# A diffusion block on one core: front reordered, stores and loads moved between queues, SiLU by Sigmoid

## The chip, the core and the metric

The kernel runs on one core of a Trainium2 chip. The metric is the device time of one execution in microseconds (us), as the median over several runs. Five engines take instructions, each strictly in its own order: PE (TensorE: matmuls, with PEld for its weight loads), DVE (VectorE: elementwise work), ACT (ScalarE: activations, casts, copies), POOL (GpSimd) and SP (SyncE, which here only issues DMAs). SP, ACT and POOL each issue DMAs into a queue of their own.

## What is computed

One layer over 512 latent tokens `x` and 256 context tokens, width 1024, fp32:

```python
m_lat = (silu(c) @ mod_w + mod_b)                  # 6 sections of 1024: sh1, sc1, g1, sh2, sc2, g2
m_ctx = (silu(c_ctx) @ mod_w + mod_b)
h_lat = rms_norm(x, g) * (1 + sc1) + sh1           # the same for ctx with csc1, csh1
qkv, a, beta, g_a, q_b, i_b, f_b, g_b, m_a, m_b = split(h @ w_in)
# mixer A: gated DeltaNet, 4 heads; mixer B: HGRN2, 4 heads; both directions, chunks of 64;
# each scan starts from the final context state
ya = (head_norm(oa) * silu(g_a)) @ w_up_a
yb = (head_norm(ob) * silu(g_b)) @ w_up_b
x = x + g1 * ((sigmoid(m_a) * ya + sigmoid(m_b) * yb) @ w_out)
x = x + g2 * swiglu(rms_norm(x) * (1 + sc2) + sh2, ffn_w_in, ffn_w_out)
return rms_norm(x, final_norm_g)
```

## The kernel before

Everything has features on the 128 partitions and tokens along the free axis. A product with full precision is three fp32r matmuls: `split` loads 128 columns of a weight as `raw` (L92, SP's queue), casts them to `hi` on ACT (L100) and takes `lo = raw - hi` on DVE (L102); `mm3` (L110) then runs hi·hi, hi·lo and lo·hi over the blocks of the contraction.

The program is written with the Tile framework: buffers come from pools with rings (`bufs`), waits are derived from data and from rings, and each engine's order follows the place in the code, moved by `tc.cur_priority`. The stages, with the times at which they stand in the profiled execution:

- Front (0 to 95 us). `x` is loaded and normed. `modulation(q)` (L279 to L293) works on two 128-feature blocks of shift and scale at a time: 16 matmuls `pmod` on two tiles `mw` (1 MB each, L279), a copy `mr` to SBUF (L282), four matmuls with `comb` that turn the rows into columns (L284), and three small DVE operations into `mcol`. For each feature block d, `px` transposes the normed rows (L299), ACT writes `hhi` (L301) and `hf` (L303) from it, and DVE `hlo` (L304). The first six M_B gates are accumulated over d in six banks `pg` (L330, weights `wr` loaded whole by SP). Then come `gate_out` for those six, two more gates (22 and 23, `pgate`), the context's `chi`, `clo` (px in the banks "ga"), and `pab` (L375), the small projections on the context.
- `gate_out` (L136, L137) copies a gate's bank to `gt` on ACT and stores it to DRAM (`gdram`) through SP's queue; the ring of `gt` has two buffers.
- Mixer (95 to 605 us). Eight generators are stepped by the string `PLAN`: G0 and G2 (DeltaNet, two heads each), H0 to H3 (HGRN2), F (a gate between them), and N or aT, one quarter of a later modulation section: `mod_early` loads 1 MB `mwe` through POOL's queue, reduces it over the eight k-blocks on DVE (L851 to L854) and sums over partitions with `column_sums` (L116, 16 matmuls). What PLAN does not place comes as `mod_quarter` (`mwb`, POOL's queue) near the end of the mixer. The heads' outputs are stored to `ydram` (L439) on SP's queue.
- Merge (605 to 720 us, its first loads from 582 us). `branch(br)` loads the gate `ug` and the head output `uy` (SP), takes SiLU on ACT (L956), multiplies on DVE (L959), splits into `yh`, `yl`. `up` multiplies with w_up (`pup`), loads the merge gate `mg` (SP, same ring "ug" of four buffers), takes its Sigmoid (L974) and multiplies with the bank (L976).
- FFN (720 to 1080 us), which the change does not touch.

## Time and profile before

| | |
|---|---|
| median of 3 runs | 1079.61 us (1078.65 to 1081.12) |
| the profiled execution | 1081.61 us, span 1079.6 us, granted TensorE clock 0.99 |
| PE, DVE, ACT, POOL busy | 94%, 61%, 51%, 7% of the span |
| DMA traffic | 122 MB, 113 GB/s on average, 290 to 329 GB/s in the first 54 us |

The profiled execution is one of its own; durations below come from it. The views used are the page (busy time, the chain of waits that ended last, groups of instructions, DMA issues), the windows (busy time of each engine in given stretches), the timeline (instructions in order of time, with the idle time ahead of each in brackets and what ended it) and the waits (who waited for whom, total, times, longest). "128*32" ahead of a matmul is the part of the array used.

### The profile page before, as it was taken

To read this page: it belongs to the slowest core of one execution; us is meant where nothing else is said; L and a number is where in the kernel's file an instruction comes from. 1 tells how busy PE (TensorE), PEld (TensorE's weight loads), DVE (VectorE), ACT (ScalarE), POOL (GpSimd) and SP (SyncE) were. 2 spreads that over 40 slices of the span, in tenths; PEclk is the share of its full clock that TensorE was granted. 3 is DMA by queue.
4 is the path that set the end of the run, shared out by engine and by line. 5 is a ranking of instruction groups with operands and counts; after the bars stand their busy time and mean duration, and the time that the engine had idled before them with its cause. 6 is when DMAs were issued, how large, how long until landed. Compare 5 with 4: busy or idle time off the path is not lost.

```text
span 1079.6 us, 16501 instructions
## 1 busy us (share of the span) xinstructions
PE 1014.1 (94%) x6455; PEld 839.9 (78%) x6455; DVE 656.5 (61%) x1238; ACT 554.5 (51%) x1042; POOL 76.6 (7%) x133
## 2 busy tenths in 40 slices
PE   4999999979999999999999899999999999999996
PEld 2686788858897877789777688797888878888785
DVE  3336886789867967976797565776343433422524
ACT  3456578748976765887774643442222222221212
POOL 1010000320002022000201000010000000000000
PEclk8999999999999999999999999999999999999999
DMA  9953412122004213200738743455333323322222
GB/s 329 290 168 91 138 55 65 54 79 59 3 11 147 64 45 88 59 2 22 241 112 280 239 159 120 137 158 174 98 97 96 96 85 98 97 97 96 86 95 95
DMA packets 134529, 122.07 MB, mean 113 GB/s; under 512 B 5533, under 2 KB 110259, under 8 KB 134451
## 3 DMA queue, kind: packets, MB, share of 16 engines
q1 hardware_dynamic: 127715, 100.20, 29.9%
q0 software_dynamic: 4640, 17.30, 4.9%
q10 hardware_dynamic: 2096, 3.50, 0.9%
q8 instruction: 51, 0.84, 0.3%
q14 instruction: 27, 0.22, 0.1%
HBM read 110.51 MB, written 10.49 MB: 112 GB/s over the span
## 4 chain that ended last, share of the span: by engine, by line
PE 60%; DVE 13%; DMA 9%; ACT 7%; issue 7%; POOL 3%; SPq 0%; POOLq 0%; ACTq 0%; DVEq 0%
PE pf L110 20%; PE pfo L110 10%; PE pg L330 3%; PE pup L110 3%; PE h_z L110 3%; PE pgate L110 2%; DMA mwb<-in_mod_w_dram 2%; DVE lo L102 2%; DMA mwe<-in_mod_w_dram 2%; PE h_zv L110 2%; DMA ug<-gdram 1%; ACT hi L100 1%; DMA gdram<-gt 1%; PE p_s_pk L801 1%; PE g_k_zl L110 1%
## 5 line engine op out<-in xcount | busy, mean ns | idle before, releaser
L100 ACT CAST hi<-raw 128x1024 fp32r<-128x1024 f32 (+1 forms) x131 | 129.7, 991 | 279.9 <-PE pf L110 97.3
L102 DVE TENSOR_TENSOR lo<-raw,hi 128x1024 fp32r<-128x1024 f32 (+1 forms) x131 | 150.5, 1150 | 172.6 <-ACT hi L100 172.2
L110 PE MATMUL pf<-hhi,lo 128*128 128x512 f32 (+1 forms) x352 | 133.8, 380 | 0.8 <-DVE lo L102 0.8
L110 PE MATMUL pf<-hhi,hi 128*128 128x512 f32 (+1 forms) x352 | 133.8, 381 | 0.0
L110 PE MATMUL pf<-hlo,hi 128*128 128x512 f32 (+1 forms) x352 | 133.7, 380 | 0.0
L110 PEld LDWEIGHTS pf<-hhi,lo 128*128 128x128 f32 x352 | 66.2, 188 | 13.7 <-DVE lo L102 1.2
L110 PEld LDWEIGHTS pf<-hlo,hi 128*128 128x128 f32 x352 | 66.2, 188 | 12.5 <-DVE hlo L1042 0.2
L110 PEld LDWEIGHTS pf<-hhi,hi 128*128 128x128 f32 x352 | 66.1, 188 | 12.5
L110 PE MATMUL pfo<-lo,uh 128*128 128x512 f32 x176 | 68.8, 391 | 0.1
L110 PE MATMUL pfo<-hi,ul 128*128 128x512 f32 x176 | 68.5, 389 | 0.0
L110 PE MATMUL pfo<-hi,uh 128*128 128x512 f32 x176 | 67.9, 390 | 0.0
L110 PE MATMUL pgate<-hhi,lo 128*128 128x512 f32 x144 | 59.2, 412 | 6.5 <-DVE lo L102 6.5
L110 PE MATMUL pgate<-hhi,hi 128*128 128x512 f32 x144 | 59.2, 411 | 2.3 <-ACT hi L100 2.3
L110 PE MATMUL pgate<-hlo,hi 128*128 128x512 f32 x144 | 58.2, 404 | 0.0
L1098 DVE TENSOR_TENSOR sg<-sg,pf 128x512 f32<-128x512 f32 x22 | 15.1, 687 | 49.3 <-PE pf L110 49.3
L835 DVE SCALAR_TENSOR_TENSOR acc<-mwb,sc,acc 128x256 f32<-128x256 f32 x72 | 34.5, 484 | 12.4 <-DMA mwb<-in_mod_w_dram 11.2
L110 PEld LDWEIGHTS pfo<-lo,uh 128*128 128x128 f32 x176 | 33.0, 188 | 7.8 <-DVE lo L102 1.0
L110 PEld LDWEIGHTS pfo<-hi,uh 128*128 128x128 f32 x176 | 32.8, 188 | 7.4 <-ACT hi L100 0.7
L110 PEld LDWEIGHTS pgate<-hhi,lo 128*128 128x128 f32 x144 | 27.8, 193 | 13.8 <-DVE lo L102 8.9
L110 PE MATMUL h_z<-hhi,hi 128*128 128x512 f32 x96 | 38.1, 397 | 0.4 <-ACT abT L376 0.3
L110 PEld LDWEIGHTS pfo<-hi,ul 128*128 128x128 f32 x176 | 33.0, 188 | 6.8
L110 PE MATMUL h_z<-hhi,lo 128*128 128x512 f32 x96 | 38.0, 396 | 0.0
(443 smaller groups left out, 2498.3 us busy)
## 6 DMA issues: line engine op xcount, KB each, us to landing
raw<-in_ffn_w_in_dram SPq DMA_DIRECT2D x44, 512.0 KB, 3.7
raw<-in_w_in_dram SPq DMA_DIRECT2D x37, 512.0 KB, 3.7
raw<-in_ffn_w_out_dram SPq DMA_DIRECT2D x22, 512.0 KB, 3.6
mwb<-in_mod_w_dram POOLq DMA_DIRECT2D x18, 512.0 KB, 4.6
mw<-in_mod_w_dram SPq DMA_DIRECT2D x16, 512.0 KB, 6.0
mwe<-in_mod_w_dram POOLq DMA_DIRECT2D x7, 1024.0 KB, 6.1
gdram<-gt SPq DMA_DIRECT2D x24, 256.0 KB, 3.3
raw<-in_w_in_dram SPq DMA_DIRECT2D x18, 256.0 KB, 2.9
```

Source lines behind the costliest of these rows:

```text
L100: nc.scalar.copy(hi[:, :, :], raw[:, :, :])
L102: nc.vector.tensor_tensor(lo[:, :, :], raw[:, :, :], hi.bitcast(F32), op=ALU.subtract)
L110: nc.tensor.matmul(ps, a[u](k), b[v](k), start=(start and n == 0), stop=(stop and n == tot - 1))
L330: nc.tensor.matmul(pg0[i][:, :], u[:, P * i:P * i + P], v[:, d, :], start=(d == 0 and n == 0), stop=(d == KT - 1 and n == 2))
L801: nc.tensor.matmul(pk[:, 2 * P:3 * P], kend[:, :], u[:, :], start=True, stop=True)
L835: nc.vector.scalar_tensor_tensor(acc[:, :], mw[:, k - k0, :], sc[:, k:k + 1], acc[:, :], op0=ALU.mult, op1=ALU.add)
L1098: nc.vector.tensor_tensor(sg[:, :], sg[:, :], pgu[1][:, :], op=ALU.mult)
```

## The change

1. Modulation comes in five groups of blocks, (0), (1), (2,3), (4,5), (6,7). The first two have one 1 MB tile with all eight k-blocks and 512-byte rows; the `comb` matmuls are four times as many, on 32 columns each. The `wr` loads stand between them.
2. Gates 22 and 23 stand behind the context's norm and `pab` in the code, with priority lowered (`+1500`) and weight tiles of their own. The context's `px` uses the banks "ha"; for odd d its `hf` is made on DVE.
3. Four quarters of the modulation that PLAN had at its start are computed in the front by `mod_now`, loaded by SP into the `mw` ring.
4. The 24 gate stores and the 8 head-output stores are issued by ACT. The `gt` ring has three buffers in the front.
5. The loads `ug` and `mg` are issued by POOL, and `mg` has a ring of four of its own.
6. SiLU is `gt*yt` on DVE, Sigmoid on ACT, and a second product on DVE.
7. The mask `lev` comes as uint8 (112 KB in place of 448) and needs no cast on ACT.

```diff
-PLAN = ("H0:1 aT:1 N:1 aT:2 G0:6 F:1 H1:3 G0:4 F:1 G2:3 G0:5 F:2 N:1 G0:1 H0:2 "
+PLAN = ("H0:1 G0:6 F:1 H1:3 G0:4 F:1 G2:3 G0:5 F:2 N:1 G0:1 H0:2 "
...
         def gate_out(i, ps, pool, tag="raw"):
-            gt = pool.tile([P, SEQ], F32, name=f"gt{i}", tag=tag, bufs=2)
+            gt = pool.tile([P, SEQ], F32, name=f"gt{i}", tag=tag, bufs=3 if pool is ring.get("sp") else 2)
             nc.scalar.copy(gt[:, :], ps[:, :])
-            nc.sync.dma_start(gdram[i, :, :], gt[:, :])
+            nc.scalar.dma_start(gdram[i, :, :], gt[:, :])
...
+        def mod_now(sec, j, mw, queue):
+            c0 = D * sec + 256 * j
+            queue.dma_start(mw[:, 0:KT, :], T["mod_w"][0, :, c0:c0 + 256].rearrange("(k p) f -> p k f", p=P))
+            for k in range(KT):
+                acc = mw[:, k % 2, :]
+                if k < 2:
+                    nc.vector.tensor_scalar_mul(acc, acc, sc[:, k:k + 1])
+                else:
+                    nc.vector.scalar_tensor_tensor(acc, mw[:, k, :], sc[:, k:k + 1], acc, op0=ALU.mult, op1=ALU.add)
+            nc.vector.tensor_tensor(mw[:, 0, :], mw[:, 0, :], mw[:, 1, :], op=ALU.add)
+            mod_sum(sec, j, mw[:, 0, :], "fa")
...
+            groups = ((0, 1), (1, 2), (2, 4), (4, 6), (6, 8))
+            def load_mod(d0, d1):
+                n, kn = P * (d1 - d0), KT // (d1 - d0)
+                for k0 in range(0, KT, kn):
+                    mw = s1.tile([P, kn, 2 * n], F32, name=f"mw{d0}_{k0}", tag="mw", bufs=6)
...
+            def modulation(d0, d1):
+                nd = d1 - d0
+                ps = bank("ha", f"pmod{d0}")
+                for k, mw in enumerate(mws[d0]):
+                    r = slice(32 * (k % 4), 32 * (k % 4) + 32)
+                    nc.tensor.matmul(ps[r, 0:2 * P * nd], sch[:, k, :], mw, start=(k < 4), stop=(k >= 4), tile_position=(0, r.start))
...
+                for i in range(2 * nd):
+                    for j in range(0, P, 32):
+                        nc.tensor.matmul(ps[j:j + 32, 2 * i:2 * i + 2], mr[:, P * i + j:P * i + j + 32], comb[:, :],
+                                         start=True, stop=True, tile_position=(0, j))
...
-            for i in rest[0:2]:
-                gate(i, sp)
             for d in range(KT):
-                normed(d, 1, (0, 1), chi, clo, "ga")
+                normed(d, 1, (0, 1), chi, clo, "ha")
...
+            tc.cur_priority += 1500
+            for i in rest[0:2]:
+                w = [s1.tile([P, KT, P], F32R, name=f"rw{i}{j}") for j in range(2)]
+                w = split([W_IN[:, gcols[i]:gcols[i] + P]], KT, P, dst=[t[:, :, :] for t in w])
+                gate_out(i, feat(w, lat, SEQ, f"pgate{i}"), sp, "gt")
+            for q in quarters[0:4]:
+                mod_now(*q, s1.tile([P, KT, 256], F32, name="mwe%d%d" % q, tag="mw", bufs=6), nc.sync)
+            del quarters[0:4]
+            tc.cur_priority -= 1500
...
-            nc.sync.dma_start(ydram[i, :, :], y)
+            nc.scalar.dma_start(ydram[i, :, :], y)
...
-                    nc.sync.dma_start(gt[:, :], gdram[4 * br + h, :, :])
-                    nc.scalar.activation(gt[:, :], gt[:, :], AF.Silu)
+                    nc.gpsimd.dma_start(gt[:, :], gdram[4 * br + h, :, :])
                     yt = yp.tile([P, SEQ], F32, name=f"uy{br}{h}", tag="uy", bufs=3)
                     nc.sync.dma_start(yt[:, :], ydram[4 * br + h, :, :])
+                    nc.vector.tensor_tensor(yt[:, :], gt[:, :], yt[:, :], op=ALU.mult)
+                    nc.scalar.activation(gt[:, :], gt[:, :], AF.Sigmoid)
                     nc.vector.tensor_tensor(yt[:, :], gt[:, :], yt[:, :], op=ALU.mult)
...
-                        gt = yp.tile([P, SEQ], F32, name=f"mg{br}{i}", tag="ug", bufs=4)
-                        nc.sync.dma_start(gt[:, :], gdram[8 + 8 * br + i, :, :])
+                        gt = yp.tile([P, SEQ], F32, name=f"mg{br}{i}", tag="mg", bufs=4)
+                        nc.gpsimd.dma_start(gt[:, :], gdram[8 + 8 * br + i, :, :])
```

How the order moves is shown at three places. A row is the line of the code, the operation, the tiles written and read (with running numbers that differ between the two programs) and the size.

PE in the front, before, from the first modulation group to the first projection matmuls (`pmod` is modulation, `px` the transposes of block d, `pg_0` to `pg_5` the six gates):

```order
L279 MATMUL pmod_216<-mw_114,sch 32x512 x4
L299 MATMUL px_237<-sq,xt_106 128x128
L299 MATMUL px_237<-sq,xt_108 128x128
L299 MATMUL px_237<-sq,xt_110 128x128
L279 MATMUL pmod_216<-mw_117,sch 32x512 x4
L299 MATMUL px_237<-sq,xt_112 128x128
L284 MATMUL pmod_216<-comb,mr_225 128x2 x4
L330 MATMUL pg_0_210<-hhi,wh_234 128x512
L330 MATMUL pg_1_211<-hhi,wh_234 128x512
```

The same place after the change:

```order
L310 MATMUL pmod_216<-mw_0_117,sch 32x256 x8
L331 MATMUL px_241<-sq,xt_106 128x128
L331 MATMUL px_241<-sq,xt_108 128x128
L331 MATMUL px_241<-sq,xt_110 128x128
L331 MATMUL px_241<-sq,xt_112 128x128
L315 MATMUL pmod_216<-comb,mr_225 32x2 x8
L310 MATMUL pmod_251<-mw_0_121,sch 32x256 x8
L366 MATMUL pg_0_210<-hhi,wh_238 128x512
L331 MATMUL px_276<-sq,xt_106 128x128
L331 MATMUL px_276<-sq,xt_108 128x128
```

The first group needs one tile where it needed two; the second group's `pmod`, its transposes and its `comb` matmuls now stand ahead of all but the first projection matmul of d = 0.

ACT behind the projection, before (`gt` copies of the six gates and, between them, casts of later weights; the context's first `chi` and `hf` at the end):

```order
L100 CAST hi_566<-raw_564 128x1024
L136 COPY gt_546<-pg_0_210 128x512
L136 COPY gt_549<-pg_1_211 128x512
L100 CAST hi_600<-raw_598 128x1024
L136 COPY gt_552<-pg_2_212 128x512
L136 COPY gt_555<-pg_3_213 128x512
L100 CAST hi_826<-raw_824 128x1024
L136 COPY gt_558<-pg_4_214 128x512
L136 COPY gt_561<-pg_5_215 128x512
L136 COPY gt_595<-pgate_570 128x512
L100 CAST hi_981<-raw_979 128x1024
L301 ACTIVATE chi<-px_632,mcol 128x256
```

After the change:

```order
L136 COPY gt_608<-pg_0_210 128x512
L136 COPY gt_611<-pg_1_211 128x512
L137 DMA gdram<-gt_608 128x512
L137 DMA gdram<-gt_611 128x512
L136 COPY gt_614<-pg_2_212 128x512
L333 ACTIVATE chi<-px_626,mcol 128x256
L137 DMA gdram<-gt_614 128x512
L136 COPY gt_617<-pg_3_213 128x512
L136 COPY gt_620<-pg_4_214 128x512
L137 DMA gdram<-gt_617 128x512
L137 DMA gdram<-gt_620 128x512
L136 COPY gt_623<-pg_5_215 128x512
```

The stores stand among the copies on ACT itself, the first `chi` has moved up between them, and the two gates' copies (`pgate`) come later.

The loads of the branch gates, before, on SP (`ug` gates, `uy` head outputs, `mg` merge gates, with the last gate stores among them):

```order
L955 DMA ug_6150<-gdram 128x512
L958 DMA uy_6153<-ydram 128x512
L955 DMA ug_6158<-gdram 128x512
L137 DMA gdram<-gt_5664 128x512
L958 DMA uy_6161<-ydram 128x512
L955 DMA ug_6166<-gdram 128x512
L958 DMA uy_6169<-ydram 128x512
L955 DMA ug_6174<-gdram 128x512
L973 DMA mg_6201<-gdram 128x512
```

After, on POOL (`mwb` are the last loads of the late modulation):

```order
L876 DMA mwb_5647<-in_mod_w_dram 128x4x256
L980 DMA ug_6210<-gdram 128x512
L876 DMA mwb_5653<-in_mod_w_dram 128x4x256
L980 DMA ug_6219<-gdram 128x512
L980 DMA ug_6228<-gdram 128x512
L980 DMA ug_6237<-gdram 128x512
L999 DMA mg_6265<-gdram 128x512
L999 DMA mg_6282<-gdram 128x512
L999 DMA mg_6343<-gdram 128x512
L980 DMA ug_6288<-gdram 128x512
```

The gate loads stand behind the modulation's last loads on POOL, and no longer between stores and head outputs on SP.

More of the change, by code (lines that the diff above doesn't have):

```diff
@@ L40, in shape_constants @@
     lev = [(r // (2 * b) == c // (2 * b)) & (r // b != c // b) for b in LEVELS]
[L41 removed]
+    return sq, np.concatenate(lev, axis=1).astype(np.uint8)
 def view(ap, offset, dims):
@@ L151, in gate_low, with mod_sum @@
             gate_out(i, ps, pool)
+        quarters = [(sec, j) for sec in (2, 3, 4) for j in range(4)]
+        def mod_now(sec, j, mw, queue):
[9 more added lines that the diff above has]
+            mod_sum(sec, j, mw[:, 0, :], "fa")
+        def mod_sum(sec, j, acc, tag):
+            ps = bank(tag, f"pmo{sec}{j}")
+            for i in range(2):
+                column_sums(ps, i, acc[:, P * i:P * i + P])
+            c = 8 * sec + 2 * j
+            nc.vector.tensor_tensor(mbc[:, c:c + 2], ps[:, 0:2], mbc[:, c:c + 2], op=ALU.add)
         NG0 = 6
@@ L906, in filler @@
                     gate_low(gates.pop(0), fl)
-        quarters = [(sec, j) for sec in (2, 3, 4) for j in range(4)]
         before, after = PLAN.split("X")
```

88 lines of the change are left out of this document (33 added, 55 removed).

## The prediction

> **What bounds the kernel now.** I read the page first, for the engine that carries the end.
>
> ```profile
> PE 1014.1 (94%) x6455; PEld 839.9 (78%) x6455; DVE 656.5 (61%) x1238; ACT 554.5 (51%) x1042; POOL 76.6 (7%) x133
> PE 60%; DVE 13%; DMA 9%; ACT 7%; issue 7%; POOL 3%; SPq 0%; POOLq 0%; ACTq 0%; DVEq 0%
> ```
>
> PE is busy for 1014 of 1079.6 us. The change takes hardly any matmul away, so it can win only PE's idle time, some 65 us, and time at a lowered clock. DMA is 9% of the chain that ended last, though it is no bound on average: some stages wait for transfers. So I read the windows by stage (columns: stretch, length, busy time and instructions of PE, PEld, DVE, ACT, POOL, granted clock, DMA share, GB/s).
>
> ```profile
> 13.00:20.00 7.00, 5.27 (x28) 2.07 (x28) 1.53 (x5) 1.66 (x2) 0.00 (x0) 1.00 1.08 363
> 20.00:26.00 6.00, 4.58 (x11) 3.61 (x12) 2.05 (x4) 1.45 (x2) 0.00 (x0) 0.50 1.08 366
> 37.00:70.00 33.00, 33.00 (x176) 23.94 (x175) 12.71 (x24) 16.84 (x25) 3.56 (x8) 1.00 0.58 183
> 70.00:95.00 25.00, 22.38 (x111) 16.51 (x109) 8.61 (x21) 15.70 (x31) 0.16 (x2) 0.93 0.60 181
> 95.00:134.00 39.00, 37.31 (x298) 31.57 (x298) 33.43 (x83) 19.93 (x31) 2.22 (x10) 0.96 0.37 109
> 134.00:560.00 426.00, 401.92 (x3335) 343.43 (x3326) 335.13 (x703) 313.52 (x676) 51.09 (x81) 1.00 0.23 70
> 605.00:631.00 26.00, 21.73 (x174) 16.94 (x174) 14.69 (x25) 13.03 (x19) 0.00 (x0) 1.00 0.70 222
> ```
>
> What may be won: the start before 37 us, of which 6 us run at clock 0.50; then 2.6 us idle and 7% of clock in 70 to 95; 1.7 us and 4% in 95 to 134; 4.3 us in 605 to 631. From 37 to 70 PE has no gap: whatever arrives sooner there moves everything behind it. In the long mixer stretch PE idles 24 us, but the change offers it nothing there.
>
> **Part 1, the modulation in five groups.** The timeline of the front (start, duration; in brackets the idle time ahead and what ended it):
>
> ```profile
> 13.25 1.93 PE L279 MATMUL pmod<-mw,sch 128*32 128x512 f32 x8 [7.43 <-DVE xt L270]
> ...
> 16.22 1.20 PE L279 MATMUL pmod<-mw,sch 128*32 128x512 f32 x8 [0.21 <-DMA mw<-in_mod_w_dram]
> ...
> 20.59 0.78 ACT L301 ACTIVATE hhi<-px,mcol 128x512 fp32r<-128x512 f32 x1 [1.64 <-DVE mcol L293]
> ...
> 21.42 2.93 PE L330 MATMUL pg<-hhi,wh 128*128 128x512 f32 x6 [2.13 <-ACT hhi L301]
> ...
> 37.00 1.07 PE L330 MATMUL pg<-hhi,wh 128*128 128x512 f32 x4
> ```
>
> The first group waits for its second megabyte until 16.2 us; at 363 GB/s 1.05 MB takes 2.9 us, so after the change its weights are there near 13.3, when the normed x releases PE anyway. From 16.22 to the first `hhi` it took 4.4 us; with half as many columns but twice as many `comb` matmuls the first `hhi` comes near 18.9 (13.3, plus some 1.2 for `pmod`, plus that chain). Then, however, PE's order puts the second group's `pmod`, four `px` and `comb` ahead of five of the six first projections, so dense work starts near 21.1, hardly before 21.42. What is won lies in what follows: in before, the first two blocks took 15.6 us up to 37.0, of which 5.6 us lay in the stretch at clock 0.50, which costs 2.8 us. If PE has no such stretch, block 2 starts at 21.1 + 12.8 = 33.9, a gain of 3.1; if it has, at 36.5, a gain of 0.5. The second group's matmuls fill the 2.13 us hole ahead of 21.42, so I lean to the former: **−2.5 us** (0 to −3.5). The Trainium skill ("TensorE: Matmul & The Clock Gate", Part 1) says that the array halves its clock after an idle window of about 3.4 us and returns after about as long a busy one. The trace fits (7.43 us idle, then holes, then 0.50), and by the rule a start with holes stays cold: the gain would be 0.5, a sum of −7.7.
>
> **Part 2, gates behind the context, third buffer, stores on ACT, uint8 mask.** The chain of waits from the end of the projection (start, duration, link):
>
> ```profile
> 69.46 0.60 ACT gt L136
> ...
> 70.07 4.02 DMA gdram<-gt
> ...
> 74.78 3.39 DMA gdram<-gt
> ...
> 79.72 4.43 DMA gdram<-gt
> ...
> 93.45 0.74 PE h_z L110 x2
> ```
>
> and the groups of ACT in that stretch (count, then busy time and mean ns):
>
> ```profile
> L301 ACT ACTIVATE chi<-px,mcol 128x256 fp32r<-128x256 f32 x8 | 4.6, 571 | 0.1
> L100 ACT CAST hi<-raw 128x1024 fp32r<-128x1024 f32 x4 | 4.2, 1053 | 2.0 <-PE pg L330 1.5 <-PE pgate L110 0.4
> ```
>
> The first copy starts near 69.5, PE's projection ends near 70.2, and three round trips of the two-buffer ring follow: a copy waits for a store to land, and the context's `chi` stands behind the copies on ACT. To the first mixer matmul (`h_z`, 93.45) pass 23.3 us. In the new order a store still takes its round trip, but only from the fourth copy on, and the 48 matmuls of gates 22 and 23, which PE ran first, can fill its time while ACT makes `chi` and `hf`. ACT's chain from the projection's end: six copies at 0.60, eight `chi` and four `hf` at 0.57 (DVE makes the other four), two casts at 1.05, six issues at 0.4 (part 5) and some 1.7 us of waits for stores, an estimate: 16.5 us. `pab` and its columns end some 4.5 us later, near 21: **−2.3 us** (0 to −4.4, the idle 2.6 plus 7% of 25 us; a loss if the banks "ha", now the only two for `px`, hold PE for more than the 1.3 us that I count inside the 21). The `lev` cast's 0.9 us goes besides, off this chain.
>
> **Part 3, four quarters moved forward.** The chain and timeline near 128 us, and the DVE groups:
>
> ```profile
> 116.26 7.77 DMA mwe<-in_mod_w_dram
> ...
> 128.34 0.31 PE L116 MATMUL pmo<-ones,mwe 128*32 128x1 f32 x16 [1.69 <-DVE mwe L854]
> L853 DVE SCALAR_TENSOR_TENSOR mwe<-mwe,sc 128x256 f32<-128x256 f32 x42 | 17.2, 480 | 0.0
> ```
>
> A quarter costs DVE six of 0.48 us and three small ones, some 3.9 us; four are 15.7 us. In 95 to 134 DVE is 33.4 us busy of 39 and PE waits 1.69 us for a quarter behind a late load. In the front they meet a DVE that has 8.6 of 25 us in use (70 to 95) and 20 us free before. There, with 24 of 25 busy, is the risk: the third quarter's operations stand among the first `clo`. The 4 MB of loads move from POOL to SP, ahead of two `raw` loads of the mixer; at 183 GB/s in that stretch, half the rate above, there is room. **−2.4 us** (0 to −3.3, the idle and 4% of clock).
>
> **Part 4, the merge.** One link of the chain, and PE's gaps there:
>
> ```profile
> 607.31 4.16 DMA mg<-gdram
> ...
> 607.93 0.50 PE L110 MATMUL pup<-yh,hi 128*128 128x512 f32 x1 [2.26 <-DVE x L976]
> ...
> 612.34 0.50 PE L110 MATMUL pup<-yh,hi 128*128 128x512 f32 x1 [1.35 <-DVE x L976]
> ```
>
> PE waits for DVE's product with `mg` to free a bank; `mg` waits in the shared ring for a `ug` slot, lands late, and then ACT loads a table (groups of ACT and DVE):
>
> ```profile
> L974 ACT ACT_TABLE_LOAD x2 | 2.6, 1283 | 1.4 <-DMA mg<-gdram 1.4
> L956 ACT ACT_TABLE_LOAD x2 | 2.6, 1283 | 0.7 <-DMA ug<-gdram 0.7
> L959 DVE TENSOR_TENSOR uy<-ug,uy 128x512 f32<-128x512 f32 x8 | 5.4, 691 | 9.2 <-ACT ug L956 5.2 <-DMA uy<-ydram 4.0
> ```
>
> With a ring of its own `mg` is loaded while `ug` is used. Sigmoid serves both gates, so three of four table loads go (3.8 us of ACT). The second product adds 8 x 0.69 = 5.5 us to a DVE with 14.7 of 26 in use: hidden; were it not, the gain would be gone. On POOL the loads stand behind the last `mwb`, and there a load is slower:
>
> ```profile
> raw<-in_w_in_dram SPq DMA_DIRECT2D x37, 512.0 KB, 3.7
> mwb<-in_mod_w_dram POOLq DMA_DIRECT2D x18, 512.0 KB, 4.6
> ```
>
> 0.9 us for each of 24 loads, hidden when issued a load or two ahead. **−4.0 us** (0 to −4.3). The Trainium skill ("DMA: Bandwidth & Descriptors", SWDGE vs HWDGE vs iDMA) calls the software path, that is POOL's, the slower one to set up, and speaks for leaving plain loads where they are. The rows agree in sign; by it a load is late where nothing runs ahead, which would leave the sum at −5.7 if all of the merge's gain went.
>
> **Part 5, stores in ACT's order.** Prices of an issue: a store on ACT at the end of the kernel, and SP's issues of these very stores (shortest, median, longest in ns):
>
> ```profile
> 1069.77 0.37 ACTq L1136 DMA_DIRECT2D out_dram<-x  x1
> L137 SPq DMA_DIRECT2D gdram<-gt x24: 319/338/684, 70.1 to 604.9; - x24
> ```
>
> 32 stores at 0.37 plus perhaps 0.15 to see the copy done, half a microsecond, are 16 us; 24 of them, 12 us, lie in the mixer, where ACT has 112 us free. Behind each stands whatever ACT does next, and PE waits for ACT in places. All hidden is 0, all on the path at the longest issue 24 x 0.684 = +16.4. With ACT at 74% and PE never bound by it for long, I take one eighth of 12: **+1.5 us**. SP in turn is freed: its in-order stores waited there for ACT ahead of weight loads, which I price at nothing since PE hardly waited for a weight.
>
> **The sum.** −2.5 −2.3 −2.4 −4.0 +1.5 = −9.7. The profiled execution took 1081.6 us (span 1079.6), which gives 1071.9; the median of the runs shown, 1079.61, is 2.0 lower, so 1069.9, say **1070 us**.
>
> **Rivals.**
> - *Gains lost downstream* (chance 0.25). What the front wins the mixer takes back: its PE gaps are waits on DVE and ACT chains of the two recurrences, and a PE that comes 7 us sooner may wait for a weight or a chain that does not. Against it: 33 us without a gap from 37 to 70. If half of parts 1 to 3 and half of 4 goes, −4.1: 1075.5; with cases from 1072.5 to 1077.4.
> - *A larger gain* (0.12). Every term at its best end and stores free: −3.5 −4.4 −3.3 −4.3 = −15.5, 1064; and SP's queue, no longer blocked by stores, brings weights in sooner than I credit. The 24 us of PE idle in the mixer could shrink by a few more: down to 1060.
> - *Slower: ACT as the bound in the mixer* (0.10). An issue at its longest, 0.684 us, on PE's path for all 24 stores gives −11.2 + 16.4 = +5.2: 1084.8. It decides against the change from 13.4 us on the path (11.2 of gain and 2.2 of resolution), that is 0.56 us a store. For it: ACT is in order, and the chain shows ACT at 7%. Against it: ACT's 26% of free time and the 0.37 row.
> - *No effect* (0.10). Part 1 cold (−0.5), the `clo` chain behind the quarters on a DVE that is full (parts 2 and 3 cancel), loads late in the merge: 1077.5 to 1081.7.
>
> **How the numbers follow.** The forecast's own range, 1066 to 1072.5, has 0.43. Within 0.2% is 2.2 us either way, about what a measurement of this kernel can tell (the runs lie 2.5 us apart). Faster: 0.43 + 0.25 + 0.12 = 0.80; same 0.10; slower 0.10. For 8 in 10 the range takes in most of the first two rivals: 1062 to 1078, leaving out the far end of the larger gain and most of the last two.
>
> **What would show it.** Part 1: block 2's `pg` at 34 us or at 36.5, and the clock from 20 to 26. Part 2: first `h_z` some 5 us sooner than 93.45 with part 1 in it, one or two waits of `gt` for a store instead of three. Part 3: the gap at 128.34 gone. Part 4: no PE gaps at `pup` behind the product with `mg`, one table load in the merge, and `mg` landed before its Sigmoid. Part 5: ACT-queue issues near 0.4 us; PE's idle time from 134 to 560 no more than 24 + 1.5 us. Wrong would be: a DVE queue in 70 to 95 that holds `clo` back, PE idle in the mixer growing by more than 5 us with ACT as releaser, or `ug` landing later than before.

## The result and the profile after

The change made the kernel slower: 1092.41 us (median, 1090.37 to 1093.09) beside 1080.36 us for the kernel before (its profiled execution counted in), a ratio of 1.0111 [1.0095, 1.0128]. Forecast were 1070 us and a range of 1062 to 1078. The profiled execution has a span of 1091.0 us (before 1079.6) at a granted clock of 0.984 (before 0.99).

The page after (span; busy time by engine; the chain that ended last, by engine):

```profile
span 1091.0 us, 16709 instructions
PE 1022.1 (94%) x6567; PEld 842.8 (77%) x6567; DVE 663.0 (61%) x1254; ACT 547.3 (50%) x1034; POOL 86.6 (8%) x153
PE 66%; DVE 13%; ACT 7%; DMA 7%; issue 4%; POOL 2%; SPq 0%; ACTq 0%; POOLq 0%; DVEq 0%
```

PE is busy 8 us longer, though the work hardly changed (112 more records in 6567, most of them the new small `comb` matmuls): part of it runs at a lower clock, where each matmul takes longer. The windows after (stretch, length, busy time of PE, PEld, DVE, ACT, POOL, granted clock, DMA share, GB/s) answer to those shown of before; the last three rows take the mixer in pieces:

```profile
20.00:26.00 6.00, 6.00 (x42) 4.67 (x39) 2.88 (x7) 1.51 (x3) 0.00 (x0) 1.00 1.09 362
37.00:70.00 33.00, 33.00 (x224) 22.59 (x223) 16.01 (x33) 16.56 (x24) 1.21 (x2) 0.97 0.72 221
70.00:95.00 25.00, 21.79 (x119) 15.75 (x117) 17.98 (x51) 12.39 (x24) 0.54 (x10) 0.93 0.68 217
95.00:134.00 39.00, 38.02 (x296) 32.31 (x296) 22.38 (x52) 22.17 (x37) 1.56 (x5) 1.00 0.20 55
134.00:560.00 426.00, 400.36 (x3270) 340.72 (x3269) 324.20 (x679) 305.92 (x666) 49.61 (x78) 0.98 0.23 68
...
95.00:260.00 165.00, 157.07 (x1092) 131.31 (x1092) 123.49 (x243) 108.12 (x185) 18.75 (x43) 0.96 0.21 61
260.00:500.00 240.00, 223.88 (x2089) 192.87 (x2088) 179.81 (x382) 173.59 (x408) 24.47 (x32) 0.99 0.18 53
500.00:614.00 114.00, 103.05 (x613) 85.69 (x612) 85.76 (x185) 73.21 (x162) 20.69 (x28) 0.97 0.52 170
```

The same pieces before:

```profile
95.00:260.00 165.00, 155.13 (x1109) 129.35 (x1109) 132.30 (x274) 109.45 (x184) 21.63 (x49) 0.98 0.25 73
260.00:500.00 240.00, 226.96 (x2141) 196.93 (x2140) 187.13 (x406) 177.93 (x424) 22.82 (x32) 1.00 0.17 50
500.00:600.00 100.00, 94.11 (x559) 78.98 (x558) 79.34 (x162) 68.74 (x146) 13.86 (x16) 1.00 0.61 193
```

The stretch from 20 to 26 us and the one around the 128 us gap are better than before, 37 to 95 us a little worse. The loss lies behind: in 260 to 500 PE does 52 matmuls fewer in the same time (2089 and 2141 in the records), and the last piece, which also takes in what was late by 500, is 14 us longer. The stages are bounded by the first uses of `h_z` (mixer) and `pup` (merge). In these rows stand the shortest, median and longest duration in ns, then the first and the last start, here before:

```profile
L110 PE MATMUL h_z<-hhi,hi x96: 387/389/501, 93.4 to 532.4; 128*128 128x512 f32 x96
...
L110 PE MATMUL pup<-yh,hi x64: 389/389/504, 600.1 to 651.5; 128*128 128x512 f32 x64
```

and after:

```profile
L110 PE MATMUL h_z<-hhi,hi x96: 387/389/504, 95.0 to 538.2; 128*128 128x512 f32 x96
...
L110 PE MATMUL pup<-yh,hi x64: 389/389/504, 614.8 to 662.7; 128*128 128x512 f32 x64
```

Stage by stage, from the first use of `h_z`, `pup` and `pwo` (after the merge), with "idle" as the stretch less PE's busy time and "lost clock" as length times (1 − granted clock), summed over windows of 1 us:

| | before | after |
|---|---|---|
| first `h_z` | 93.4 | 95.0 |
| mixer, `h_z` to `pup` | 506.7 | 519.8 |
| merge, `pup` to `pwo` | 52.1 | 48.6 |
| PE idle, mixer | 28.8 | 35.0 |
| lost clock, mixer | 3.4 | 11.9 |
| PE idle, whole span | 65.5 | 68.8 |
| lost clock, whole span | 11.0 | 17.4 |

So the merge won 3.5 us, the front lost 1.6, and the mixer, which the prediction left out of its sum, lost 13.1, more by clock than by idle time. All these figures are of one execution of each kernel; executions of one kernel lie 3 us apart here, and up to 12 in the runs below. The largest waits of PE in 95 to 620 (total us, times, longest) after:

```profile
PE pgate L110 <- ACT hi L100: 7.2, 6, 2.9
PE p_pt L480 <- ACT p_on L477: 5.3, 2, 3.9
PE pgate L110 <- DVE lo L102: 4.4, 3, 2.3
```

and the same three before (L437 is L480 of after):

```profile
PE pgate L110 <- DVE lo L102: 6.5, 5, 2.9
...
PE p_pt L437 <- ACT p_on L434: 2.9, 2, 1.9
...
PE pgate L110 <- ACT hi L100: 2.3, 4, 0.9
```

The waits are of the same kinds, for a weight's cast or for the recurrences' chains, but in other places; these three sum to 16.9 us after and 11.7 before.

### The profile page after: what moved, and what is told of

It reads as the page before. It is cut to its first block, busy times and chain, and to the rows that moved or that the text cites. A ratio compares the mean times of both kernels' runs of the same rounds, so it can differ in the third digit from the quotient of the medians.

```text
span 1091.0 us, 16709 instructions
## 1 busy us (share of the span) xinstructions
PE 1022.1 (94%) x6567; PEld 842.8 (77%) x6567; DVE 663.0 (61%) x1254; ACT 547.3 (50%) x1034; POOL 86.6 (8%) x153
## 4 chain that ended last, share of the span: by engine, by line
PE 66%; DVE 13%; ACT 7%; DMA 7%; issue 4%; POOL 2%; SPq 0%; ACTq 0%; POOLq 0%; DVEq 0%
PE pf L110 20%; PE pfo L110 10%; PE pgate L110 4%; PE h_z L110 4%; PE pg L366 3%; PE pup L110 3%; DVE lo L102 2%; PE g_q_zl L110 2%; DMA mwb<-in_mod_w_dram 2%; PE h_pA L531 2%; PE g_k_zl L110 1%; PE p_pD L707 1%; ACT hi L100 1%; PE p_s_pk L844 1%; PE g_v_zl L110 1%
## 5 line engine op out<-in xcount | busy, mean ns | idle before, releaser
L100 ACT CAST hi<-raw 128x1024 fp32r<-128x1024 f32 (+1 forms) x129 | 127.5, 990 | 272.0 <-PE pf L110 96.2
L102 DVE TENSOR_TENSOR lo<-raw,hi 128x1024 fp32r<-128x1024 f32 (+1 forms) x129 | 147.9, 1147 | 170.7 <-ACT hi L100 170.5
L110 PE MATMUL pfo<-lo,uh 128*128 128x512 f32 x176 | 68.8, 391 | 0.1
L110 PE MATMUL pgate<-hhi,hi 128*128 128x512 f32 x128 | 54.0, 422 | 7.2 <-ACT hi L100 7.2
L110 PE MATMUL pgate<-hhi,lo 128*128 128x512 f32 x128 | 54.1, 423 | 4.5 <-DVE lo L102 4.4
L110 PE MATMUL pgate<-hlo,hi 128*128 128x512 f32 x128 | 53.2, 415 | 0.0
L878 DVE SCALAR_TENSOR_TENSOR acc<-mwb,sc,acc 128x256 f32<-128x256 f32 x72 | 34.5, 482 | 16.6 <-DMA mwb<-in_mod_w_dram 15.3
L110 PE MATMUL h_z<-hlo,hi 128*128 128x512 f32 x96 | 38.2, 398 | 0.0
```

The costliest lines, as they stand in the source:

```text
L100: nc.scalar.copy(hi[:, :, :], raw[:, :, :])
L102: nc.vector.tensor_tensor(lo[:, :, :], raw[:, :, :], hi.bitcast(F32), op=ALU.subtract)
L110: nc.tensor.matmul(ps, a[u](k), b[v](k), start=(start and n == 0), stop=(stop and n == tot - 1))
L878: nc.vector.scalar_tensor_tensor(acc[:, :], mw[:, k - k0, :], sc[:, k:k + 1], acc[:, :], op0=ALU.mult, op1=ALU.add)
```

## The experiments

### Which part carries the loss

The first four undo or isolate one part. The ratios are to runs of the kernel before taken beside them. Loads of the gates back on SP:

```diff
-                    nc.gpsimd.dma_start(gt[:, :], gdram[4 * br + h, :, :])
+                    nc.sync.dma_start(gt[:, :], gdram[4 * br + h, :, :])
...
-                        nc.gpsimd.dma_start(gt[:, :], gdram[8 + 8 * br + i, :, :])
+                        nc.sync.dma_start(gt[:, :], gdram[8 + 8 * br + i, :, :])
```

> The changed kernel with the branch gates' and merge gates' loads (ug, mg) issued by SP again; the rings stay as changed and PE's order is the same instruction for instruction. Theory 1 (late loads): in the changed kernel the first ug is issued on POOL behind the last modulation loads, lands at 601.4 us, and ACT, which stands at its Sigmoid, holds back the cast for the last rest gate, so that PE idles 3.7 us and then runs 3.4 us' worth of cold clock ahead of the first up-projection (614.8). With the loads on SP the first ug lands some 8 us sooner, the first up-projection starts near 607 and the kernel takes 1084 to 1087 instead of 1092.4. Theory 2 (stores on ACT) and theory 3 (the order of the mixer): the tail is only where an earlier delay shows, and the time stays within 2 us of 1092.

Measured: 1.0100 [1.0071, 1.0129], mixer 519.1 us. PE's order is the same as after the change; moved alone, the loads are not the loss.

All 32 stores back on SP:

```diff
-            nc.scalar.dma_start(gdram[i, :, :], gt[:, :])
+            nc.sync.dma_start(gdram[i, :, :], gt[:, :])
...
-            nc.scalar.dma_start(ydram[i, :, :], y)
+            nc.sync.dma_start(ydram[i, :, :], y)
```

> The changed kernel with the gate and head-output stores issued by SP again. Theory 2 (stores in ACT's order cost the mixer): 24 issues at 0.33 us no longer stand ahead of casts and activations, the idle time and the cold stretches between 95 and 500 us go back to those of before, and the time falls by 5 us or more, to 1087 or less. Theories 1 and 3: it stays within 2 us of 1092, since ACT is idle a quarter of the mixer and an issue of 0.33 us is short.

Measured: 1.0033 [1.0015, 1.0051]. Two thirds of the loss go. The first `h_z` comes at 86.8 us instead of 95.0, and the mixer takes 514.9 us instead of 519.8.

The four quarters back in PLAN, on POOL's queue:

```diff
-PLAN = ("H0:1 G0:6 F:1 H1:3 G0:4 F:1 G2:3 G0:5 F:2 N:1 G0:1 H0:2 "
+PLAN = ("H0:1 aT:1 N:1 aT:2 G0:6 F:1 H1:3 G0:4 F:1 G2:3 G0:5 F:2 N:1 G0:1 H0:2 "
...
-            for q in quarters[0:4]:
-                mod_now(*q, s1.tile([P, KT, 256], F32, name="mwe%d%d" % q, tag="mw", bufs=6), nc.sync)
-            del quarters[0:4]
```

> The changed kernel with the four early modulation quarters back at the start of the mixer's plan and on POOL's queue, all else as changed. Theory 3 (without the quarters the streams stand differently against each other, PE waits for casts near 217 and 230 us and goes cold): the cold stretches of 216 to 234 and 338 to 344 go, some 6 us, and the time falls to about 1086 although the 1.7 us stall near 128 may come back. Theories 1 and 2: 1092, or up to 2.4 us more.

Measured: 1.0038 [1.0019, 1.0058]; first `h_z` 90.0, mixer 515.8. This too takes two thirds off. Two thirds twice is more than there is to take: the parts don't add.

On the kernel before, the merge's part alone (Sigmoid and a second product, `mg` in a ring of its own, loads still on SP):

```diff
-                    nc.scalar.activation(gt[:, :], gt[:, :], AF.Silu)
...
+                    nc.vector.tensor_tensor(yt[:, :], gt[:, :], yt[:, :], op=ALU.mult)
+                    nc.scalar.activation(gt[:, :], gt[:, :], AF.Sigmoid)
...
-                        gt = yp.tile([P, SEQ], F32, name=f"mg{br}{i}", tag="ug", bufs=4)
+                        gt = yp.tile([P, SEQ], F32, name=f"mg{br}{i}", tag="mg", bufs=4)
```

> The kernel before with the merge's parts alone: SiLU as product, Sigmoid, product, and a ring of four of its own for the merge gates; all loads stay on SP. If the ring and the missing table loads are what took the PE gaps out of the up-projections (4.3 us idle before, 1.0 after the change), the kernel takes 1076 to 1077 against 1080. If the gaps went because the loads come from another queue, it stays at 1080.

Measured: 0.9985 [0.9967, 1.0003], not told apart from 1. In its trace the merge takes 50.0 us (before 52.1), PE idles 2.0 us there (4.3), and the mixer is unchanged at 506.7.

### Single parts on the kernel before

The stores alone on ACT:

```diff
-            nc.sync.dma_start(gdram[i, :, :], gt[:, :])
+            nc.scalar.dma_start(gdram[i, :, :], gt[:, :])
...
-            nc.sync.dma_start(ydram[i, :, :], y)
+            nc.scalar.dma_start(ydram[i, :, :], y)
```

> The kernel before with one part of the change: all gate and head-output stores are issued by ACT. Theory 2 (the stores in ACT's order cost by themselves): the front loses several us (in the changed kernel ACT's copies wait up to 4.4 us for a store, and putting the stores back on SP moved the first mixer matmul from 95.0 to 86.8), and the mixer some; 1085 to 1090. Theory 4 (stores and the quarters' loads hurt only together, since the two 1 MB loads of SP run while the stores of ACT want the DMA engines): alone the stores cost under 2 us, 1080 to 1083.

Measured: 1.0123 [1.0085, 1.0161]: two words of code cost as much as the whole change. The four quarters in the front, alone, loaded by SP into the `mw` ring:

```diff
-PLAN = ("H0:1 aT:1 N:1 aT:2 G0:6 F:1 H1:3 G0:4 F:1 G2:3 G0:5 F:2 N:1 G0:1 H0:2 "
+PLAN = ("H0:1 G0:6 F:1 H1:3 G0:4 F:1 G2:3 G0:5 F:2 N:1 G0:1 H0:2 "
...
+            for q in quarters[0:4]:
+                mw = s1.tile([P, 4, 512], F32, name="mwe%d%d" % q, tag="mw", bufs=6)
+                mod_now(*q, mw[:, :, :].rearrange("p k (j n) -> p (k j) n", j=2), nc.sync)
+            del quarters[0:4]
```

> The kernel before with one part of the change: the four early modulation quarters are computed at the end of the front, loaded by SP, and the plan loses them. My prediction: -2.4 us, 1078, with the stall at 128 us and its cold stretch gone. Theory 3 (without the quarters in it, the mixer's streams are ordered otherwise, with more waits of over 2 us and a cold stretch behind each): the front gains little and the mixer, first h_z to first up-projection, grows from 506.7 us by 4 or more; 1083 to 1087.

Measured: 1.0065 [1.0034, 1.0097], mixer 515.2. The five groups alone, with `load_mod` and `modulation` as changed:

```diff
+            groups = ((0, 1), (1, 2), (2, 4), (4, 6), (6, 8))
...
-            for d in range(KT):
-                load_mod(d)
+            for d0, d1 in groups:
+                load_mod(d0, d1)
```

> The kernel before with one part of the change: the modulation in five groups. In the changed kernel the projection ended at 69.5 us against 70.2, so of the 2.5 us predicted 0.7 came. Alone it should give the same 0.7 us or up to 2.5 and leave the order of the mixer nearly as it was: 1078 to 1080. If the new order of the front moves the mixer too, the mixer's length departs from 506.7 by more than 3 us.

Measured: 1.0007 [0.9986, 1.0029], first `h_z` 91.6, no lost clock in the front, mixer 508.6: the front's 1.8 us are used up by a mixer 1.9 us longer. And the changed kernel with the stores on SP and the quarters in PLAN together, where each had taken two thirds off:

> The changed kernel with both undone: stores on SP and the four quarters back in the mixer's plan on POOL (groups, gates behind the context, uint8 mask, loads on POOL and Sigmoid stay). Each alone gave back some 8 of the 11 us. If they are one cause (theory 4, stores that wait behind the quarters' loads) both together give no more than one: 1084 to 1087. If they are two causes that add, the kernel comes to 1077 to 1080, with the first h_z near 85 us and a mixer of under 512.

Measured: 1.0147 [1.0110, 1.0185], worse than either and than the change itself; mixer 526.2. Costs of instructions do not behave so.

What does is the order. In the traces of before and `b_stores_act`, with buffer numbers left out and a run of equal instructions as one row, 444 of PE's 4396 rows stand elsewhere, 195 of DVE's 989 and 169 of ACT's 879, though only the queue of 32 stores is another. One piece of PE's difference, in the mixer (`h_pA` and `p_pYb`, `p_pRb` are steps of the two recurrences, `g_k_zl`, `g_k_zc` projections that fill):

```order
 L746 MATMUL p_pX_2496<-p_T_2300 32x32
 L760 MATMUL p_pRb_2711<-p_X_2303,p_N 64x64 x12
+L488 MATMUL h_pA_3162<-h_kq_3157 128x128 x2
+L110 MATMUL g_k_zl<-hlo,hi_3503 128x512
+L110 MATMUL g_k_zl<-hhi,lo_3505 128x512
+L766 MATMUL p_pYb_2712<-p_N,p_T_2299 64x64 x6
+L766 MATMUL p_pYb_2712<-p_N,p_T_2300 64x64 x6
```

Only the new rows (+) are shown; in before seven matmuls of `g_k_zc` stand between `p_pRb` and `p_pYb`. The same steps now have other work ahead of them, and so wait in other places.

### The order held

The next kernels keep an edit but hold the instructions in the order of before, each one behind its predecessor on the same engine, by dependencies that set the order and put in no semaphore:

```diff
+        _by = {i.name: i for i in nc.cur_bb.bb.instructions}
+        for _s in _j.loads(_z.decompress(_b.b85decode(ORDER))):
+            for _p, _q in zip(_s, _s[1:]):
+                tc.add_manual_dep(_by["I-%d" % _q], "I-%d" % _p, mybir.DependencyInfo(
+                    mybir.DependencyClass.NoSync, mybir.DependencyReason.DATA), reason="order")
```

`ORDER` holds, for each engine, the numbers of its instructions in before's order.

In `b_stores_pin` all of before's instructions on all five engines but the stores are held so, and the stores are on ACT:

> The kernel before with all stores issued by ACT, as in b_stores_act (1.2% slower), but with every other instruction of all five engines held in the order of the kernel before, by dependencies that only fix the order. Theory 2 (the stores cost by standing in ACT's order): it stays near 1095. Theory 5 (the scheduler's new order of the mixer is what costs; the move of a store only sets it off): the mixer, first h_z to first up-projection, is again within 3 us of 506.7 and the kernel takes 1079 to 1083; at most the front keeps a loss.

Measured: 0.9996 [0.9978, 1.0015], against 1.0123 for the same stores without the hold. First uses in `b_stores_act` (ns shortest, median, longest; first to last start):

```profile
L110 PE MATMUL h_z<-hhi,hi x96: 387/389/504, 96.6 to 540.9; 128*128 128x512 f32 x96
...
L110 PE MATMUL pup<-yh,hi x64: 387/389/504, 618.2 to 668.0; 128*128 128x512 f32 x64
```

in `b_stores_pin`:

```profile
L110 PE MATMUL h_z<-hhi,hi x96: 387/389/497, 93.7 to 532.1; 128*128 128x512 f32 x96
...
L110 PE MATMUL pup<-yh,hi x64: 389/389/504, 600.3 to 650.9; 128*128 128x512 f32 x64
```

and the issues of its gate stores on ACT, by their line:

```profile
L137 ACTq DMA_DIRECT2D gdram<-gt x24: 326/326/355, 70.7 to 605.0; - x24
```

The mixer takes 521.6 us in the one and 506.6 in the other, with the same 0.33 us issues; of the 15.0 us, 9.8 are idle time of PE and 5.1 lost clock. These two executions lie somewhat further apart than the kernels (1098.4 and 1079.6, medians 1096.3 and 1083.8). No row of DVE or ACT and only two of PE's differ from before's order in the trace of `b_stores_pin`. So the order costs the 1.2%, and the issues by themselves nothing that can be measured; the interval leaves room for 1.6 us. The same for the quarters on before:

> The kernel before with the four quarters in the front (0.65% slower as scheduled), the mixer held in the order of the kernel before less the quarters' instructions. Theory 5: the stall at 128 us and its cold stretch, 3.4 us, go and nothing comes in their place: 1076 to 1079. Theory 3 in its narrow form (the quarters are missing as filler): mixer still over 511, 1084 or more.

Measured: 0.9981 [0.9959, 1.0002] against 1.0065; mixer 507.8 against 515.2. Then the changed kernel whole, with the mixer's instructions that both have in before's order:

> The changed kernel as it is, with the mixer's instructions (first head to last head, gates between them included) held in the order in which the kernel before has them; front, merge and FFN are scheduled as in the changed kernel. Theory 5 (order): the mixer comes back from 519.8 to 504 to 509 us, the first h_z stays at 95, the merge keeps its 3.5 us: 1076 to 1080. If the mixer's loss is due to what the change does there (stores on ACT, quarters taken out, loads on POOL), the time stays above 1088.

Measured: 1.0065 [1.0044, 1.0086] against 1.0111; mixer 514.3 against 519.8. The hold takes some 40% of the loss away, so the order is not all of it. With the stores on SP besides:

> The changed kernel with the stores on SP (first h_z at 86.8 us, mixer 514.9) and the mixer in the order of the kernel before. Theory 5: first h_z at 87, mixer 503 to 509, merge as changed: 1066 to 1072, faster than both kernels. Without theory 5: 1085 as without the order held.

Measured: 0.9974 [0.9949, 0.9998] against 1.0033 for `a_stores_sp`; mixer 507.8. With order and stores put right the loss is gone, and a little is won.

### What is left beside the order

In `a_pin` two things stand out, the front and the end of the mixer. A theory for the end was that Sigmoid in place makes DVE's product and ACT's read wait for each other; so Sigmoid got a tile of its own in `a_pin`:

```diff
-                    nc.scalar.activation(gt[:, :], gt[:, :], AF.Sigmoid)
-                    nc.vector.tensor_tensor(yt[:, :], gt[:, :], yt[:, :], op=ALU.mult)
+                    sg = yp.tile([P, SEQ], F32, name=f"us{br}{h}", tag="us", bufs=2)
+                    nc.scalar.activation(sg[:, :], gt[:, :], AF.Sigmoid)
+                    nc.vector.tensor_tensor(yt[:, :], sg[:, :], yt[:, :], op=ALU.mult)
```

> The changed kernel with the mixer's order of before (a_pin, 0.65% slower than before, with 514.3 us from the first h_z to the first up-projection against 506.7), and the merge's Sigmoid written to a tile of its own, so that it waits for ug's load alone and no longer for DVE's product gt*yt to have read ug. In a_pin ACT stood 6.8 us at that Sigmoid with a rest gate's cast behind it, and PE idled 2.0 us and then ran cold. If that is what is left of the loss (theory 6): the stretch falls to 507 to 511 and the kernel takes 1081 to 1086 where a_pin took 1090. If the loads on POOL or the stores on ACT make the tail late, it stays at 513 or more.

Measured: 1.0087 [1.0060, 1.0114], mixer 516.8, no better than `a_pin`. That theory fell: the Sigmoid no longer waits for the product, but ACT's next cast, `yh`, does (2.58 us, until 600.91), and the weight's cast still stands behind it. The front: in `a_pin`, the gate stores of the front alone on SP:

```diff
-            nc.scalar.dma_start(gdram[i, :, :], gt[:, :])
+            (nc.sync if pool is ring.get("sp") else nc.scalar).dma_start(gdram[i, :, :], gt[:, :])
```

> The changed kernel with the mixer's order of before, and only the front's eight gate stores issued by SP; the 16 later gate stores and the 8 head-output stores stay on ACT. If the front's loss comes from stores that stand on ACT among copies and land late beside the quarters' two 1 MB loads, the first h_z comes at 86 to 88 us against 93.4 in a_pin, and the kernel takes 1080 to 1084, all other stages as in a_pin. If not, the first h_z stays near 93.

Measured: 1.0019 [1.0001, 1.0037] against 1.0065; first `h_z` 89.2 against 93.4. In `a_pin` three of ACT's copies wait 5.3 us in all for stores, in `a_pin_fst` none. The same is seen in the changed kernel, with `a_stores_sp` beside it. The chain after the change, from the projection's end:

```profile
69.30 0.60 ACT gt L136
...
71.22 6.81 DMA gdram<-gt
78.05 0.59 ACT gt L136
...
95.04 0.90 PE h_z L110 x3
```

The timeline of SP and ACT there:

```profile
67.28 2.10 SPq L158 DMA_DIRECT2D mwe<-in_mod_w_dram  x2
...
76.00 0.59 ACT L136 COPY gt<-pg 128x512 f32<-128x512 f32 x1 [4.35 <-DMA gdram<-gt]
```

and that of the copies in `a_stores_sp`:

```profile
67.05 1.56 ACT L136 COPY gt<-pg 128x512 f32<-128x512 f32 x3 [3.43 <-PE pg L366]
71.69 0.63 ACT L136 COPY gt<-pg 128x512 f32<-128x512 f32 x1
72.62 1.14 ACT L136 COPY gt<-pg 128x512 f32<-128x512 f32 x2
```

SP issues two quarters' loads, 1 MB each, from 67.28 on; the third store, issued on ACT at 71.22, lands 6.8 us later. The fourth copy waits 4.35 us, until 76.00, for the first copy's buffer to be stored. With the stores in SP's own queue three of them stand ahead of the first of these loads, the six copies are done by 73.8 us, and none of them waits for a store.

The run `best`, that is `a_stores_sp` with a Sigmoid tile of its own and the order held, was to put both together; the gate loads are still on POOL:

> What the experiments point to: the changed kernel with its stores on SP, the mixer in the order of the kernel before, and the Sigmoid in a tile of its own. Without the last step it was 0.26% faster than before. Expected: first h_z at 87, 504 to 508 us to the first up-projection, merge 49 to 52: 1072 to 1078 where before takes 1082, that is 0.4 to 0.9% faster. If theory 6 is wrong, 0.2 to 0.3% as without the step.

Measured: 0.9983 [0.9963, 1.0002], mixer 511.5: no better than before, and no better than `a_stores_sp_pin`.

The end of the mixer, then, in `a_pin`. The timeline of POOL and ACT:

```profile
584.84 2.15 POOL L980 DMA_DIRECT2D ug<-gdram  x4
586.98 1.60 POOL L999 DMA_DIRECT2D mg<-gdram  x3
...
598.17 0.63 ACT L984 ACTIVATE ug<-ug 128x512 f32<-128x512 f32 x1 [6.82 <-DVE uy L983]
```

and one link of the chain:

```profile
585.43 11.92 DMA uy<-ydram
```

POOL issues seven loads of 256 KB in 3.8 us, and the head output that SP asked for at 585.43 lands 11.9 us later; from 588 to 596 us the DMA engines are full (share 1.03 to 1.08, 355 to 412 GB/s). ACT stands 6.8 us behind it, since Sigmoid waits for the product with it, and ACT's next weight cast stands behind the Sigmoid. So the loads in `a_pin` went to SP, among the others:

> The changed kernel with the mixer's order of before and the loads ug and mg issued by SP, where they alternate with the head outputs uy. In a_pin POOL issued four ug and four mg, 2 MB, between 584.8 and 590 us; the first uy, issued by SP at 585.4 into the same DMA engines, landed 11.9 us later, and DVE's product, ACT's Sigmoid and the casts of the last rest gate stood behind it. Theory 7 (the early burst of gate loads on a second queue delays uy): first h_z to first up-projection falls from 514.3 to 507 to 510 us, 1083 to 1087. If it stays at 513 or more, the queue of the loads isn't the cause and the tail stays open.

Measured: 1.0040 [1.0021, 1.0060] against 1.0065 [1.0044, 1.0086], mixer 511.8 against 514.3: part of it, and with intervals that overlap. Last, stores and gate loads on SP, the mixer's order held, the rest as changed:

> The changed kernel with stores and gate loads on SP and the mixer in the order of before; the front, uint8 mask, own ring for mg and Sigmoid stay as changed (the Sigmoid in place). With the loads on POOL this was 0.26% faster than before. Theory 7: first h_z at 87 us, 503 to 507 to the first up-projection, 1073 to 1078 where before takes 1081: 0.3 to 0.7% faster. If theory 7 is wrong: 0.2 to 0.3% faster as with the loads on POOL.

Measured: **0.9915 [0.9888, 0.9942]**, 1073.15 us (1071.89 to 1076.03) beside 1084.0 (1077.82 to 1090.19): faster than both kernels. First uses in it:

```profile
L110 PE MATMUL h_z<-hhi,hi x96: 387/389/499, 88.4 to 526.9; 128*128 128x512 f32 x96
...
L110 PE MATMUL pup<-yh,hi x64: 387/389/497, 596.6 to 645.0; 128*128 128x512 f32 x64
```

Front 5.0 us shorter than before, mixer 508.2 (before 506.7), merge 49.1 (52.1). It differs from `a_stores_sp_pin` in the gate loads alone, PE's order is the same, and the two intervals do not meet, though only just, and the two ratios are to different runs of before. So with the stores on SP these loads on POOL seem to cost some 0.6%. The profiles do not show where (spans 1074.2 and 1074.3; that of `a_stores_sp_pin` was its fastest execution). With the stores on ACT the same move gave 0.25% in `a_pin_loads` and 0.1% in `a_loads_sp`, neither told apart from nothing.

## Why the prediction was wrong

The step that failed is the sentence "In the long mixer stretch PE idles 24 us, but the change offers it nothing there", and with it every part's assumption that the 500 us of mixer are executed as before. The change reorders them, and the mixer took 519.8 us where 506.7 was taken for granted: the hold alone brings some 13 us back in `b_stores_pin` (1.0123 to 0.9996) and some 5 us in the changed kernel itself (1.0111 to 1.0065). The rest is gone once the stores are on SP as well (0.9974), and the gate loads on SP win a little more (0.9915). The rival "gains lost downstream" named the mixer, but priced it only as gains not kept, 1077.4 at most, not as a mixer longer than before.

- **Part 1** (−2.5): the wait for the second megabyte is gone, and 20 to 26 us now stand at clock 1.00, so that stretch is not "cold" as the alternative had it. But block 2 came at 35.3, not 33.9, and the stretch at half clock lies further on:

```profile
13.67 1.93 PE L310 MATMUL pmod<-mw,sch 128*32 128x256 f32 x16 [7.98 <-DMA mw<-in_mod_w_dram]
...
18.29 1.94 PE L310 MATMUL pmod<-mw,sch 128*32 128x256 f32 x16 [1.07 <-DMA mw<-in_mod_w_dram]
...
35.31 2.26 PE L366 MATMUL pg<-hhi,wh 128*128 128x512 f32 x5 [1.64 <-ACT hhi L333]
```

  The second group waits 1.07 us for its weights and the rest of the first projection starts at 22.05, not 21.1. The 1.64 us wait is followed by the 0.97 of 37 to 70: from 36 to 39 us the clock is 0.50. The projection ended 0.6 us earlier. By itself (`b_groups`) the first `h_z` came 1.8 us sooner, inside the range given, though the kernel was no faster. By the prediction's own figures the cold case is 21.1 + 15.6 = 36.7, a gain of 0.3 and not 0.5. The prediction's remark that the trace fits (7.43 us idle, then holes, then 0.50) is not what the rows say: 13 to 20 us stand at 1.00 right behind the 7.43 us. The durations leave it open, since eight such `pmod` take 1.93 us at 13.25, 1.20 at 16.22 and 1.06 at 27.75.
- **Part 2** (−2.3): wrong in sign with the stores on ACT (`h_z` 95.0); with them on SP, which is not what was predicted, it is 86.8 (`a_stores_sp`), where −2.5 −2.3 from 93.4 gives 88.6. The 1.7 us of waits for stores counted in its 16.5 were 5.2 (4.35, 0.47 and 0.40 in ACT's timeline); with the 1.9 us that part 1 lacked this makes 5.4 of the 6.4 us between 88.6 and 95.0. Part 3's loads and part 2's stores were each priced alone and met on the DMA engines (share 1.02 to 1.10 from 68 to 80 us).
- **Part 3** (−2.4): the gap at 128 us is gone and PE is busy 38.0 of 39 us at full clock there (37.3 at 0.96): locally 0.7 idle and 1.6 of clock, 2.3 in all. The order that came with it costs more (`b_quarters` 1.0065, held 0.9981).
- **Part 4** (−4.0): the merge is 3.5 us shorter, PE's idle time in it 1.0 us instead of 4.3, and one table load is left. What was missed stands ahead of the merge, in the last 40 us of the mixer. The table load among the groups of ACT after the change (count, busy time, mean ns, idle time ahead):

```profile
L984 ACT ACT_TABLE_LOAD x1 | 1.3, 1283 | 8.2 <-DMA ug<-gdram 8.2
```

  a link of the chain there:

```profile
592.70 8.68 DMA ug<-gdram
```

  and PE's timeline just behind it, then a window on the same stretch:

```profile
604.84 0.50 PE L110 MATMUL pgate<-hhi,hi 128*128 128x512 f32 x1 [2.04 <-ACT hi L100]
...
607.23 0.80 PE L110 MATMUL pgate<-hhi,lo 128*128 128x512 f32 x1 [1.65 <-DVE lo L102]
```

```profile
606.00:612.00 6.00, 4.77 (x11) 3.80 (x12) 4.89 (x8) 4.51 (x9) 1.54 (x3) 0.50 0.66 217
```

  ACT waits 8.2 us for `ug`, and the cast of the last gate's weight stands behind it in ACT's order; PE then waits twice and runs at half clock. "Hidden when issued a load or two ahead" did not hold here, where POOL's loads come in a burst and the DMA engines are full (share 1.04 from 598 to 602 us): the median `ug` landed after 6.1 us, before after 4.6. The warning of the Trainium skill ("DMA: Bandwidth & Descriptors", SWDGE vs HWDGE vs iDMA) on POOL's queue, weighed there with −5.7 for the sum, pointed the right way: the loads on SP are worth some 0.6% in the held kernel with its stores on SP. The traces show a late landing behind a burst; a longer set-up they do not show.
- **Part 5** (+1.5): the price of an issue was right, 0.33 us for 0.37. What 24 of them cost on the path cannot be told from nothing (`b_stores_pin`, at most 1.6 us), so neither can the 1.5. The rival "ACT as the bound in the mixer" gave 1084.8 by issues on PE's path; that the kernel got slower there was right, the mechanism was not. From 134 to 560 PE's idle time grew by 1.6 us (25.6 for 24.1), about what the prediction allowed. Over the whole mixer it grew by 6.2, of which 3.8 in gaps that ACT ended (16.6 to 20.4). The larger part, 8.5 us, is lost clock, which the sum had only as a gain; with 1.6 us less work of PE in the mixer, these make its 13.1.

What stays open: why the mixer of `a_pin_loads` still takes 5 us more than before's, where `best2`, with the stores on SP, takes 1.5 more; and no rule tells which of the orders is a good one, since `a_st_q`, with fewer edits, got the worst mixer (that it is its order was not tested by a hold).

## What to carry to other kernels

Where a scheduler sets the order, moving a DMA to another engine's queue or a block to another place can change hundreds of places on PE, DVE and ACT, as here, and that can outweigh the edit's own price: compare the orders of the long stretches too, not only near the edit, and hold the order to measure the edit alone. When an edit seems to cost or win much more than its instructions can, suspect the order first; that two edits undone together are worse than either is a sign of it. Price a store or load by what else is on the DMA engines at that moment, and keep transfers that free buffers in one queue with the bulk loads they compete with, where their order can be set.

## What the hardware showed

Waits of 2 to 3 us of PE cost more than their length in some places. After the change, the wait ahead of 217.24 (timeline) was followed by 8 us at half clock (the window under it); the clock fell during the wait, since 216 to 217 stands at 0.77:

```profile
217.24 0.80 PE L110 MATMUL pgate<-hhi,lo 128*128 128x512 f32 x1 [2.27 <-DVE lo L102]
```

```profile
218.00:226.00 8.00, 8.00 (x78) 7.06 (x77) 5.85 (x21) 2.07 (x3) 1.80 (x4) 0.50 0.14 35
```

In `a_stores_sp_pin` a longer wait at the same gate was not:

```profile
219.53 0.50 PE L110 MATMUL pgate<-hhi,lo 128*128 128x512 f32 x1 [2.90 <-DVE lo L102]
```

```profile
222.00:226.00 4.00, 3.39 (x13) 2.10 (x12) 3.74 (x10) 1.83 (x4) 0.05 (x2) 1.00 0.73 195
```

The Trainium skill ("TensorE: Matmul & The Clock Gate", Part 1) halves the clock after an idle window of about 3.4 us; the first wait is shorter than that and was followed by the low clock. In the two us ahead of the wait PE was 74% busy in the first case and all the time in the second; two cases do not make a rule, and why the one and not the other is not settled.

When a store of 256 KB lands depends on what else is under way. The DMA issues of the stores (KB each, median us to landing), after:

```profile
gdram<-gt ACTq DMA_DIRECT2D x24, 256.0 KB, 3.1
```

and in `a_stores_sp`, with the same stores on SP:

```profile
gdram<-gt SPq DMA_DIRECT2D x24, 256.0 KB, 2.1
```

The queue alone does not set it: before, with the stores on SP, the median is 3.3 us, and in `a_quarters_back`, with the stores on ACT but without the quarters' loads in the front, it is 2.0 and the longest 2.1, where after the change the longest is 7.1.
